# A decoder block on one core: fetching down rows block by block, four native score tiles, and row rings in two

## The chip, the cores and the metric

The kernel runs on one core of a Trainium2 chip. The metric is the time of one execution on the device in microseconds. Three runs of the kernel before took 2116.78, 2117.88 and 2124.81 us; the median is 2117.88.

## The reference

The layer has 256 tokens of 2048 features in fp32. An input projection feeds windowed attention and retention; gated, merged and projected, they are added to the residual `h`. What follows is the part that matters here, the retrieval of experts:

```
hn  = RMSNorm(h)
s   = (hn @ w_query) . sub_keys          # 8 heads, 2 halves, 128 keys each
top 16 of each half -> 256 sums -> best 16: 128 expert numbers ib and gates gb per token
u   = expert_down[ib]; act = gelu(hn . u)           # 16384 experts, rows of 2048
y   = sum over the 128 experts of gb * act * expert_up[ib]
out = RMSNorm(h + y)
```

## The kernel before, in words

Tokens lie on the partitions, in two blocks `b` of 128 (`NB`). Weights come in units of up to four 128 x 512 chunks through a ring of three `raw` tiles (queue of SyncE). For an fp32r product a unit is split: ScalarE casts it to `whi`, VectorE subtracts that into `wlo` (L107, L108), and TensorE multiplies three times per chunk and block (L138 to L140, L154 to L156). Each of these rings has three slots, so splits run at most three pairs of chunks ahead of TensorE.

After `w_out` come four query tiles (`w_q`), whose scores TensorE transposes and multiplies with the sub-keys (L498, L503). Then come 32 *score tiles* (`gemm1`, L463): each multiplies 512 expert rows with all tokens, over the first 11 of the 16 feature chunks only, 8 in fp32r and 3 in native fp32 from `raw` itself (L161, `htf` is the unsplit input). ScalarE scales the result into `a` (L467) and writes it to a score table in DRAM, `a_dram` (L468).

The last 5 chunks, 640 features, are not computed for all experts. When the experts of a token are known, GpSimd (POOL) fetches 640-feature pieces of their down rows with indirect DMAs, one row per token at a time (`fetch_u`, L605), and VectorE forms the dot product (`dot`, L613, `djunk`). There are 256 such steps, 128 per block. They need the routing of a block: `top16`, `candidates`, `cand_top`, `ranks` and `pick` on VectorE give the numbers `sel`, and `indices` (L586) turns them into row numbers `ix`. Before, `indices` runs once for both blocks. Each dot frees a slot of the ring of eight tiles `v` and issues the fetch eight further on; the last eight dots issue the first fetches of *up rows* (`fetch`, L583), which use the same ring.

What runs between the tiles is put on a list by `later` with a cost; `drain` takes entries off it when a unit of a product has been written, up to a budget for that unit (`BG_RATE`, `BG_NATIVE`). A scheduler then orders the instructions of each engine by a simulated timeline. On the chip each engine takes its list in that order.

In the last stage POOL gathers, per step, one score per token from `a_dram` (`score`, L640, `wsel`) and fetches an up row of 2048 features (L583); VectorE adds gate x gelu x row into `ys` (L689). Fourteen scores lead; the order of POOL's instructions is written out by `in_line`. `finish` normalises a block.

Of the kernel before, what the change touches and what calls it, by code (L numbers as in the profile page):

```python
# [26 lines left out]
NE = 16384  # L27
NT = NE // 512
BG_RATE = 2.8
BG_NATIVE = 4.9  # L30
CF = 8
CN = 3
CG = NC - CF - CN
GC = CG * P
G0 = D - GC
DOT = 0.85
VR = 8
GRP = 8
LEAD = 14

# [2 lines left out]
def hybrid_block(ctx, tc, x, x_t, anorm, fnorm, frow, w_in, w_ab, w_rb, w_out, w_q, skeys, down, down_n, down_g, up, sinks, fin,  # L43
# [24 lines left out]
        for j in range(4):  # L68
            units += [w[j, u] for u in range(4)]
    for t in range(NT):  # L70
        units += [down[t, u] for u in range(CF // 4)] + [down_n[t]]

    state = {"emitted": 0, "used": 0}
    bg = deque()
# [1 line left out]
    def later(cost, fn, *args):  # L76
        bg.append((cost, fn, args))
# [8 lines left out]
    ready = {}  # L86

    def emit_unit(u):
        if units[u].shape[1] == CN:
            nat = stream.tile([P, 4, 512], F32, name="raw", bufs=3)  # L90
            nc.sync.dma_start(nat[:, :CN], units[u])
            ready[u] = nat
            return
        raw = stream.tile([P, 4, 512], F32, name="raw", bufs=3)
        if u == 0:
            for i in range(4):
                nc.sync.dma_start(raw[:, i], units[u][:, i])
        else:
            nc.sync.dma_start(raw, units[u])
        hs = []  # L100
        for i in range(2):
            hi = stream.tile([P, 2, 512], F32R, name="whi", bufs=3)
            lo = stream.tile([P, 2, 512], F32R, name="wlo", bufs=3)
            step = 1 if u == 0 else 2
            for k in range(0, 2, step):
                src = raw[:, 2 * i + k:2 * i + k + step]
# [36 lines left out]

    def gemm_mixed(ops, xf):
        ps = [acc.tile([P, 512], F32, name="acc") for _ in range(NB)]
        for u in range(CF // 4):
            hs = next_unit()
            for k in range(4):
                hi, lo = hs[k // 2]
                wh, wl = hi[:, k % 2], lo[:, k % 2]  # L150
                c = u * 4 + k
                for b in range(NB):
                    xh, xl = ops(c, b)
                    nc.tensor.matmul(ps[b], lhsT=xh, rhs=wh, start=(c == 0), stop=False)  # L154
                    nc.tensor.matmul(ps[b], lhsT=xh, rhs=wl, start=False, stop=False)  # L155
                    nc.tensor.matmul(ps[b], lhsT=xl, rhs=wh, start=False, stop=False)  # L156
            drain(BG_RATE)
        nat = next_unit()
        for k in range(CN):
            for b in range(NB):  # L160
                nc.tensor.matmul(ps[b], lhsT=xf[:, k, b * P:(b + 1) * P], rhs=nat[:, k], start=False,  # L161
                                 stop=(k == CN - 1))
        drain(BG_NATIVE)
        return ps

    def pair_ops(hi, lo):
# [287 lines left out]

    peer = pool("peer")
    h_ops = pair_ops(hth, htl)
    htf = peer.tile([P, CN, T], F32, name="htf")
# [110 lines left out]
    for b in range(NB):  # L568
        later(2.0, candidates, b)
        for hd in range(8):  # L570
            later(1.0, cand_top, b, hd)
        later(2.0, ranks, b)
        later(4.6, pick, b, 0)
        later(4.6, pick, b, 1)
    ix = peer.tile([P, 2, NB, P], U32, name="ix")
    vtiles = {}
    vp = {}

    def fetch(n):
        v = vp["pool"].tile([P, D], F32, name="v", bufs=VR)  # L580
# [5 lines left out]
    def indices():  # L586
        rt.close()
        msk.close()
        tmp2 = pool("tmp2")
        ef = tmp2.tile([P, 2, NB, P], F32, name="ef")  # L590
        nc.vector.scalar_tensor_tensor(ef[:, 0], sel[:, 0], 128.0, sel[:, 1], op0=OP.mult, op1=OP.add)
        for b in range(NB):
            nc.vector.tensor_scalar_add(ef[:, 1, b], ef[:, 0, b], rows[:, b:b + 1])
        nc.vector.tensor_copy(ix, ef)
        vp["pool"] = pool("v")
        vp["ps"] = pool("ysum", space=PSUM)
        for n in range(VR):
            fetch_u(n)

    utiles = {}  # L600

    def fetch_u(n):
        u = vp["pool"].tile([P, D], F32, name="v", bufs=VR)
        b, k = divmod(n, P)
        nc.gpsimd.indirect_dma_start(u[:, :GC], None, down_g, IndirectOffsetOnAxis(ap=ix[:, 0, b, k:k + 1], axis=0),  # L605
                                     bounds_check=NE - 1)
        utiles[n] = u

    def dot(n):
        u = utiles.pop(n)  # L610
        b, k = divmod(n, P)
        junk = peer.tile([P, GC], BF16, name="djunk", bufs=2)
        nc.vector.scalar_tensor_tensor(junk, u[:, :GC], rstd2[:, b:b + 1], hg[:, b], op0=OP.mult, op1=OP.mult,  # L613
                                       accum_out=sdot[:, b, k:k + 1])
# [11 lines left out]
    fbc = peer.tile([P, D], F32, name="fbc")  # L626
    nc.scalar.dma_start(fbc, bass.AP(tensor=fin.tensor, offset=fin.offset, ap=[[0, P], [1, D]]))
# [67 lines left out]


# [62 lines left out]
```

## Time and profile before

| | us |
|---|---|
| median of three runs | 2117.88 |
| profiled execution | 2116.2 |
| its span, first to last instruction | 2114.4 |
| TensorE / VectorE / POOL busy | 1387.9 / 1556.2 / 918.4 |
| score tiles, first to last matmul | 873 to 1412 |
| down-row fetches, first to last issue | 963.2 to 1389.6 |
| last stage, first score issue to end | 1422 to 2114 |

Busy times are sums over the whole span. What an engine's time is worth differs from stage to stage, so the rows below are mostly of stretches. A busy TensorE is not TensorE at its peak: durations of matmuls overlap, and their pace is read from the distance of their starts.

### The profile page before, as it was taken

To read this page: it belongs to the slowest core of one execution; us is meant where nothing else is said; L and a number is where in the kernel's file an instruction comes from. 1 tells how busy PE (TensorE), PEld (TensorE's weight loads), DVE (VectorE), ACT (ScalarE), POOL (GpSimd) and SP (SyncE) were. 2 spreads that over 40 slices of the span, in tenths; PEclk is the share of its full clock that TensorE was granted. 3 is DMA by queue.
4 is the path that set the end of the run, shared out by engine and by line. 5 is a ranking of instruction groups with operands and counts; after the bars stand their busy time and mean duration, and the time that the engine had idled before them with its cause. 6 is when DMAs were issued, how large, how long until landed. Compare 5 with 4: busy or idle time off the path is not lost.

```text
span 2114.4 us, 18649 instructions
## 1 busy us (share of the span) xinstructions
PE 1387.9 (66%) x5864; PEld 1076.1 (51%) x5864; DVE 1556.2 (74%) x2037; ACT 614.7 (29%) x780; POOL 918.4 (43%) x802
## 2 busy tenths in 40 slices
PE   8999999999999999999999999960000000000000
PEld 6888888888888888866666676640000000000000
DVE  5676576544544567796777877748989899999998
ACT  6555444444444454433333333310000001000001
POOL 0101001000000000006888888857777777777773
PEclk9999999999999999999999999985555555555555
DMA  8545545655555564559999999987999999999997
GB/s 313 183 151 176 175 144 197 221 197 187 193 189 192 191 231 162 176 194 325 406 406 391 391 408 408 396 353 271 395 397 395 399 399 384 410 400 407 399 400 307
DMA packets 114516, 630.24 MB, mean 298 GB/s; under 512 B 21872, under 2 KB 22512, under 8 KB 54000
## 3 DMA queue, kind: packets, MB, share of 16 engines
q0 software_dynamic: 65536, 352.50, 42.3%
q1 hardware_dynamic: 38016, 253.77, 33.0%
q10 hardware_dynamic: 10864, 22.77, 2.8%
q8 instruction: 46, 0.75, 0.1%
q14 instruction: 54, 0.44, 0.1%
HBM read 610.10 MB, written 18.87 MB: 297 GB/s over the span
## 4 chain that ended last, share of the span: by engine, by line
PE 47%; DMA 20%; issue 17%; POOL 8%; DVE 8%; POOLq 0%; ACT 0%; ACTq 0%; DVEq 0%; SPq 0%
PE acc L139 13%; PE acc L138 13%; PE acc L140 13%; DMA v<-in_down_g_dram,ix 11%; DMA v<-in_up_dram,ix 6%; DVE ys L689 4%; POOL v L583 4%; POOL wsel L640 3%; PE acc L161 2%; DMA wsel<-a_dram,ix 2%; DVE wlo L108 1%; PE acc L155 1%; PE acc L156 1%; PE acc L154 1%; POOL v L605 1%
## 5 line engine op out<-in xcount | busy, mean ns | idle before, releaser
L108 DVE TENSOR_TENSOR wlo<-raw,whi 128x1024 fp32r<-128x1024 f32 (+1 forms) x426 | 526.1, 1236 | 332.9 <-ACT whi L107 332.5
L107 ACT CAST whi<-raw 128x1024 fp32r<-128x1024 f32 (+1 forms) x426 | 443.8, 1048 | 667.7 <-PE acc L140 367.5
L689 DVE SCALAR_TENSOR_TENSOR ys<-v,wsel,ys 128x2048 f32<-128x2048 f32 x254 | 598.3, 2355 | 30.8 <-DMA v<-in_up_dram,ix 23.3
L605 POOL DMA_INDIRECT v<-in_down_g_dram,ix x256 | 347.5, 1357 | 353.0 <-ACT whi L107 273.0
L640 POOL DMA_INDIRECT wsel<-a_dram,ix x256 | 259.1, 1012 | 96.4 <-issue 93.0
L583 POOL DMA_INDIRECT v<-in_up_dram,ix x256 | 260.9, 1019 | 80.7 <-issue 58.7
L613 DVE SCALAR_TENSOR_TENSOR djunk<-v,rs_r,hg 128x640 bf16<-128x640 f32 x256 | 219.2, 880 | 99.6 <-DMA v<-in_down_g_dram,ix 99.0
L139 PE MATMUL acc<-wlo,xth 128*128 128x512 f32 x736 | 291.9, 397 | 0.0
L140 PE MATMUL acc<-whi,xtl 128*128 128x512 f32 x736 | 288.2, 392 | 0.0
L138 PE MATMUL acc<-whi,xth 128*128 128x512 f32 x736 | 266.7, 394 | 9.1 <-ACT whi L107 9.1
L155 PE MATMUL acc<-wlo,hth 128*128 128x512 f32 x512 | 203.8, 398 | 13.1 <-DVE wlo L108 12.9
L156 PE MATMUL acc<-whi,htl 128*128 128x512 f32 x512 | 200.1, 391 | 0.0
L154 PE MATMUL acc<-whi,hth 128*128 128x512 f32 x512 | 191.4, 411 | 2.2 <-ACT whi L107 2.2
L681 ACT ACTIVATE wsel<-wsel 128x8 f32<-128x8 f32 x32 | 6.6, 208 | 595.9 <-DVE wsel L680 533.7
L161 PE MATMUL acc<-raw,htf 128*128 128x512 f32 x384 | 169.9, 592 | 0.0
L138 PEld LDWEIGHTS acc<-whi,xth 128*128 128x128 f32 x736 | 138.7, 189 | 38.3 <-ACT whi L107 9.5
L139 PEld LDWEIGHTS acc<-wlo,xth 128*128 128x128 f32 x736 | 138.8, 189 | 29.7 <-DVE wlo L108 1.0
L140 PEld LDWEIGHTS acc<-whi,xtl 128*128 128x128 f32 x736 | 138.8, 189 | 28.1 <-issue 0.2
L433 POOL TENSOR_TENSOR sg<-sg 128x512 f32<-128x512 f32 x8 | 14.1, 1790 | 291.8 <-DVE sg L432 291.8
L155 PEld LDWEIGHTS acc<-wlo,hth 128*128 128x128 f32 x512 | 96.1, 188 | 42.9 <-DVE wlo L108 22.2
L154 PEld LDWEIGHTS acc<-whi,hth 128*128 128x128 f32 x512 | 96.1, 188 | 33.5 <-issue 12.2
L161 PEld LDWEIGHTS acc<-raw,htf 128*128 128x128 f32 x384 | 72.7, 189 | 79.1 <-issue 76.6
(185 smaller groups left out, 1483.7 us busy)
## 6 DMA issues: line engine op xcount, KB each, us to landing
raw<-in_w_in_dram SPq DMA_DIRECT2D x91, 1024.0 KB, 4.8
raw<-in_down_dram SPq DMA_DIRECT2D x64, 1024.0 KB, 8.9
raw<-in_down_n_dram SPq DMA_DIRECT2D x32, 768.0 KB, 6.7
raw<-in_w_rb_dram SPq DMA_DIRECT2D x16, 1024.0 KB, 4.8
raw<-in_w_out_dram SPq DMA_DIRECT2D x16, 1024.0 KB, 4.8
raw<-in_w_q_dram SPq DMA_DIRECT2D x16, 1024.0 KB, 4.8
a_dram<-a ACTq DMA_DIRECT2D x32, 512.0 KB, 12.2
raw<-in_w_ab_dram SPq DMA_DIRECT2D x8, 1024.0 KB, 4.9
```

The lines of the kernel that those rows point to most:

```text
L107: nc.scalar.copy(hi[:, k:k + step], src)
L108: nc.vector.tensor_sub(lo[:, k:k + step], src, hi[:, k:k + step].bitcast(F32))
L138: nc.tensor.matmul(ps[b], lhsT=xh, rhs=wh, start=(c == 0), stop=False)
L139: nc.tensor.matmul(ps[b], lhsT=xh, rhs=wl, start=False, stop=False)
L140: nc.tensor.matmul(ps[b], lhsT=xl, rhs=wh, start=False, stop=(c == last))
L154: nc.tensor.matmul(ps[b], lhsT=xh, rhs=wh, start=(c == 0), stop=False)
L155: nc.tensor.matmul(ps[b], lhsT=xh, rhs=wl, start=False, stop=False)
L161: nc.tensor.matmul(ps[b], lhsT=xf[:, k, b * P:(b + 1) * P], rhs=nat[:, k], start=False, stop=(k == CN - 1))
L583: return nc.gpsimd.indirect_dma_start(v, None, up, IndirectOffsetOnAxis(ap=ix[:, 0, b, k:k + 1], axis=0), bounds_check=NE - 1)
L605: nc.gpsimd.indirect_dma_start(u[:, :GC], None, down_g, IndirectOffsetOnAxis(ap=ix[:, 0, b, k:k + 1], axis=0), bounds_check=NE - 1)
L640: return nc.gpsimd.indirect_dma_start(wsel[:, b, k:k + 1], None, a_flat, IndirectOffsetOnAxis(ap=ix[:, 1, b, k:k + 1], axis=0), bounds_che ...
L689: nc.vector.scalar_tensor_tensor(ys, v, w[:, kk:kk + 1], ys, op0=OP.mult, op1=OP.add)
```

## The change

Routing is finished block by block. `indices(b)` runs after each block's own picks; block 0's run starts the first fetches of down rows, and block 1's last score pieces (`held`) and routing steps are put behind it with a dot of block 0 after every second one. The row tiles are now two rings: `u`, nine slots of 640 features, and `v`, five slots of 2048, to which four more tiles (`more`, in the room of the split input) are added when the score tiles are done. The pool of `v` and the load of the final gain `fbc` are opened by `routed`, after block 1's routing.

All three units of the first four score tiles are native fp32. Of the other 28, a tile's third unit is native in 17 and split like the others in 11. For this `htf` has all 11 chunks and is summed on GpSimd. The costs and budgets on the list are set anew (`DOT`, 1.0 to 1.4 for the top-16 steps, 0.7 or 1.65 per chunk).

```diff
-BG_NATIVE = 4.9
-CF = 8
-CN = 3
+NATIVE_RATE = 1.65
+CD = 11
+ALL_NATIVE = 4
-DOT = 0.85
-VR = 8
+DOT = 0.95
+UR = 9
+VR = 5
...
+    native = set()
+    base = len(units) - 3 * NT
+    for t in range(NT):
+        kinds = range(3) if t < ALL_NATIVE else (2,) if (t - ALL_NATIVE) % 5 in (0, 2, 4) else ()
+        native.update(base + 3 * t + k for k in kinds)
...
+                    if u in native:
+                        nc.tensor.matmul(ps[b], lhsT=xf[:, c, b * P:(b + 1) * P], rhs=w[:, k], start=first, stop=last)
+                        continue
...
+            drain(n * (NATIVE_RATE if u in native else BG_RATE / 4))
...
-    nc.vector.tensor_add(htf, hth[:, CF:CF + CN].bitcast(F32), htl[:, CF:CF + CN].bitcast(F32))
+    for c in range(0, CD, 4):
+        e = min(c + 4, CD)
+        nc.gpsimd.tensor_add(htf[:, c:e], hth[:, c:e].bitcast(F32), htl[:, c:e].bitcast(F32))
...
-            later(1.0, top16, top[:, b, 4 * j + i], topi[:, b, 4 * j + i], sc[:, i])
+            item = (1.4, top16, top[:, b, 4 * j + i], topi[:, b, 4 * j + i], sc[:, i])
+            if b and j == 3:
+                held.append(item)
+            else:
+                later(*item)
...
-        u = vp["pool"].tile([P, D], F32, name="v", bufs=VR)
+        u = peer.tile([P, GC], F32, name="u", bufs=UR)
...
-        if n + VR < NB * P:
-            fetch_u(n + VR)
-        else:
-            fetch(n + VR - NB * P)
-
-    later(4.0, indices)
-    for n in range(NB * P):
+        if n + UR < NB * P:
+            fetch_u(n + UR)
+        elif 0 <= n + UR - NB * P < VR:
+            fetch(n + UR - NB * P)
+
+    def indices(b):
...
+        nc.vector.tensor_copy(ix[:, :, b], ef)
+        if b == 0:
+            for n in range(UR):
+                fetch_u(n)
...
+    done = 0
+    for b in range(NB):
+        steps = held if b else []
+        steps.append((2.0, candidates, b))
+        steps += [(1.4, cand_top, b, hd) for hd in range(8)]
+        steps += [(2.0, ranks, b), (4.6, pick, b, 0), (4.6, pick, b, 1), (1.0, indices, b)]
+        for i, st in enumerate(steps):
+            later(*st)
+            if b and i % 2:
+                later(DOT, dot, done)
+                done += 1
+    later(0.0, routed)
+    for n in range(done, NB * P):
         later(DOT, dot, n)
...
+    more = [keep.tile([P, 2, D], F32, name=f"more_{t}", tag=t) for t in ("xh", "xl")]
+    vp["more"] = [m[:, i] for m in more for i in range(2)]
...
+    for n in range(VR, VR + 4):
+        in_line(fetch, n)
...
-                if n + VR < total:
-                    in_line(fetch, n + VR)
+                if n + VR + 4 < total:
+                    in_line(fetch, n + VR + 4)
```

The scheduler's order shows three places. On POOL, from the last sums of the mixers to the start of the last stage, before:

```order
L433 TENSOR_TENSOR sg<-sg 128x512 x8
L605 DMA v<-in_down_g_dram,ix 128x640 x256
L583 DMA v<-in_up_dram,ix 128x2048 x8
L640 DMA wsel<-a_dram,ix 128x1 x15
L583 DMA v<-in_up_dram,ix 128x2048
```

and after:

```order
L440 TENSOR_TENSOR sg<-sg 128x512 x8
L467 TENSOR_TENSOR htf<-hth,htl 128x1024 x2
L467 TENSOR_TENSOR htf<-hth,htl 128x768
L602 DMA u<-in_down_g_dram,ix 128x640 x19
L594 DMA v<-in_up_dram,ix 128x2048 x5
L602 DMA u<-in_down_g_dram,ix 128x640 x237
L666 DMA wsel<-a_dram,ix 128x1 x14
L594 DMA more_xh<-in_up_dram,ix 128x2048 x2
L594 DMA more_xl<-in_up_dram,ix 128x2048 x2
L666 DMA wsel<-a_dram,ix 128x1
```

The sums for `htf` are new, five up rows have moved from behind the down rows to the 20th place, and four stand behind the leading scores.

On VectorE, the last dots (`djunk`) among the splits of weights (`wlo`), up to the first sum of the last stage, before:

```order
L613 SCALAR_TENSOR_TENSOR djunk,sdot<-v,rs_r,hg 128x640 x4
L108 TENSOR_TENSOR wlo<-raw,whi 128x1024
L613 SCALAR_TENSOR_TENSOR djunk,sdot<-v,rs_r,hg 128x640
L108 TENSOR_TENSOR wlo<-raw,whi 128x1024
L613 SCALAR_TENSOR_TENSOR djunk,sdot<-v,rs_r,hg 128x640 x3
L108 TENSOR_TENSOR wlo<-raw,whi 128x1024 x2
L680 TENSOR_TENSOR wsel<-wsel,sdot 128x8
L682 TENSOR_TENSOR wsel<-wsel,sel 128x8
L687 TENSOR_SCALAR ys<-v,wsel 128x2048
```

and after:

```order
L610 SCALAR_TENSOR_TENSOR djunk,sdot<-u,rs_r,hg 128x640 x6
L115 TENSOR_TENSOR wlo<-raw,whi 128x1024
L610 SCALAR_TENSOR_TENSOR djunk,sdot<-u,rs_r,hg 128x640
L115 TENSOR_TENSOR wlo<-raw,whi 128x1024
L610 SCALAR_TENSOR_TENSOR djunk,sdot<-u,rs_r,hg 128x640 x3
L115 TENSOR_TENSOR wlo<-raw,whi 128x1024 x3
L115 TENSOR_TENSOR wlo<-raw,whi 128x512
L115 TENSOR_TENSOR wlo<-raw,whi 128x1024 x13
L115 TENSOR_TENSOR wlo<-raw,whi 128x512
L115 TENSOR_TENSOR wlo<-raw,whi 128x1024 x4
L708 TENSOR_TENSOR wsel<-wsel,sdot 128x8
```

The last dot has moved from in front of the last two splits to in front of the last 22; counted from the end, these are the splits of tiles 28 to 31 (18) and four of the six of tile 27.

On TensorE, in the first score tile, the last query scores (`qs`, `sk`) among its products, before (the end of the piece):

```order
L155 MATMUL acc<-wlo,hth 128x512
L156 MATMUL acc<-whi,htl 128x512
L154 MATMUL acc<-whi,hth 128x512
L155 MATMUL acc<-wlo,hth 128x512
L156 MATMUL acc<-whi,htl 128x512
L154 MATMUL acc<-whi,hth 128x512
L155 MATMUL acc<-wlo,hth 128x512
L156 MATMUL acc<-whi,htl 128x512
L161 MATMUL acc<-raw,htf 128x512 x6
L503 MATMUL ms<-sk,qt 128x128 x4
L154 MATMUL acc<-whi,hth 128x512
L155 MATMUL acc<-wlo,hth 128x512
```

and after (the whole piece):

```order
L162 MATMUL acc<-raw,htf 128x512 x10
L507 MATMUL ms<-ident,qs 128x128 x4
L162 MATMUL acc<-raw,htf 128x512 x10
L512 MATMUL ms<-sk,qt 128x128 x4
L507 MATMUL ms<-ident,qs 128x128 x4
L162 MATMUL acc<-raw,htf 128x512 x10
L512 MATMUL ms<-sk,qt 128x128 x4
L162 MATMUL acc<-raw,htf 128x512 x54
L166 MATMUL acc<-whi,hth 128x512 x2
```

The transposes and key products of the query scores have moved in between native matmuls.

## Rows read from the trace of the kernel before

**Rows 1.** Busy time by stage (us, counts), the columns in the first row.

```profile
core 0: us, PE busy (x) PEld busy (x) DVE busy (x) ACT busy (x) POOL busy (x), PEclk, DMA share, GB/s
873.00:963.00 90.00, 87.78 (x344) 62.21 (x343) 81.17 (x268) 34.35 (x41) 0.00 (x0) 1.00 0.58 190
963.00:1398.00 435.00, 421.94 (x1553) 289.99 (x1552) 331.62 (x615) 141.06 (x156) 353.33 (x261) 1.00 1.01 397
1413.00:1442.00 29.00, 0.00 (x0) 0.00 (x0) 6.66 (x5) 1.52 (x3) 15.21 (x16) 0.54 0.24 92
1442.00:2088.00 646.00, 0.00 (x0) 0.00 (x0) 598.54 (x328) 13.04 (x44) 494.32 (x489) 0.50 1.01 397
```

**Rows 2.** Chain that ended last, share of the span by line.

```profile
PE acc L139 13%; PE acc L138 13%; PE acc L140 13%; DMA v<-in_down_g_dram,ix 11%; DMA v<-in_up_dram,ix 6%; DVE ys L689 4%; POOL v L583 4%; POOL wsel L640 3%; PE acc L161 2%; DMA wsel<-a_dram,ix 2%; DVE wlo L108 1%; PE acc L155 1%; PE acc L156 1%; PE acc L154 1%; POOL v L605 1%
```

**Rows 3.** ScalarE's timeline (start us, us, operation): results of tiles 6 and 31.

```profile
993.94 0.69 ACT L467 ACTIVATE a<-acc,rs_r 128x512 f32<-128x512 f32 x1 [6.78 <-PE acc L161]
...
1411.48 0.69 ACT L467 ACTIVATE a<-acc,rs_r 128x512 f32<-128x512 f32 x1 [11.40 <-PE acc L161]
1412.34 0.69 ACT L467 ACTIVATE a<-acc,rs_r 128x512 f32<-128x512 f32 x1 [0.17 <-PE acc L161]
```

**Rows 4.** TensorE's timeline in tile 0, fp32r and native.

```profile
880.62 0.39 PE L155 MATMUL acc<-wlo,hth 128*128 128x512 f32 x1
...
881.75 0.39 PE L154 MATMUL acc<-whi,hth 128*128 128x512 f32 x1
...
885.85 5.31 PE L161 MATMUL acc<-raw,htf 128*128 128x512 f32 x12
891.00 1.05 PE L503 MATMUL ms<-sk,qt 128*128 128x128 f32 x8
```

**Rows 5.** Tile v: ns min/median/max, first and last start us.

```profile
L605 POOL DMA_INDIRECT v<-in_down_g_dram,ix x256: 1007/1307/2168, 963.2 to 1389.6; - x128
L613 DVE SCALAR_TENSOR_TENSOR djunk<-v,rs_r,hg x256: 869/880/908, 971.5 to 1397.0; 128x640 bf16<-128x640 f32 x128
L583 POOL DMA_INDIRECT v<-in_up_dram,ix x256: 1000/1010/1641, 1391.0 to 2086.7; - x128
```

**Rows 6.** POOL's timeline: first fetch, one beside splits, first score, last stage.

```profile
963.22 2.17 POOL L605 DMA_INDIRECT v<-in_down_g_dram,ix  x1 [273.05 <-ACT whi L107]
...
1311.58 1.84 POOL L605 DMA_INDIRECT v<-in_down_g_dram,ix  x1 [0.30 <-DVE djunk L613]
...
1422.22 1.02 POOL L640 DMA_INDIRECT wsel<-a_dram,ix  x1 [18.69 <-issue]
...
1606.68 1.01 POOL L640 DMA_INDIRECT wsel<-a_dram,ix  x1 [0.30 <-issue]
```

**Rows 7.** Line 154, first and last start.

```profile
L154 PE MATMUL acc<-whi,hth x512: 387/389/793, 873.1 to 1406.3; 128*128 128x512 f32 x171
```

**Rows 8.** Groups of the page: a sum on POOL.

```profile
L433 POOL TENSOR_TENSOR sg<-sg 128x512 f32<-128x512 f32 x8 | 14.1, 1790 | 291.8 <-DVE sg L432 291.8
```

**Rows 9.** ScalarE's timeline: block 0's last query scores.

```profile
883.07 0.59 ACT L505 COPY sc<-ms 128x512 f32<-128x512 f32 x1
```

**Rows 10.** Busy time of all engines while VectorE routes.

```profile
884.00:962.20 78.20, 75.98 (x283) 52.26 (x282) 75.82 (x264) 27.04 (x33) 0.00 (x0) 1.00 0.58 188
```

**Rows 11.** Busy time of VectorE's splits (L108) in that stretch.

```profile
884.00:962.20 78.20, 20.81 (x18) 1.00 0.58 188
```

**Rows 12.** Busy time in ten microseconds, the fastest among the dots.

```profile
1200.00:1210.00 10.00, 9.44 (x38) 6.82 (x37) 9.22 (x19) 2.28 (x3) 8.17 (x7) 1.00 1.02 418
```

**Rows 13.** Groups of the page: splits on VectorE.

```profile
L108 DVE TENSOR_TENSOR wlo<-raw,whi 128x1024 fp32r<-128x1024 f32 (+1 forms) x426 | 526.1, 1236 | 332.9 <-ACT whi L107 332.5
```

**Rows 14.** VectorE's timeline beside that fetch.

```profile
1311.31 1.22 DVE L108 TENSOR_TENSOR wlo<-raw,whi 128x1024 fp32r<-128x1024 f32 x1
```

**Rows 15.** Result writes, from issue to landing.

```profile
DMA to landing us min/median/max: 6.4/12.2/14.6
```

**Rows 16.** Busy time of POOL's down-row fetches (L605) among the dots.

```profile
963.00:1398.00 435.00, 347.51 (x256) 1.00 1.01 397
```

More of the change, by code (lines that the diff above doesn't have):

```diff
@@ L70, in hybrid_block @@
     for t in range(NT):
-        units += [down[t, u] for u in range(CF // 4)] + [down_n[t]]
+        units += [down[t, 0], down[t, 1], down_n[t]]
+    native = set()
[3 more added lines that the diff above has]
+        native.update(base + 3 * t + k for k in kinds)
     state = {"emitted": 0, "used": 0}
@@ L88, in emit_unit @@
     def emit_unit(u):
[L89 to L93, printed above, removed]
         raw = stream.tile([P, 4, 512], F32, name="raw", bufs=3)
+        n = units[u].shape[1]
         if u == 0:
@@ L98, in emit_unit @@
         else:
-            nc.sync.dma_start(raw, units[u])
+            nc.sync.dma_start(raw[:, :n], units[u])
+        if u in native:
+            ready[u] = raw
+            return
         hs = []
-        for i in range(2):
+        for i in range(0, n, 2):
             hi = stream.tile([P, 2, 512], F32R, name="whi", bufs=3)
             lo = stream.tile([P, 2, 512], F32R, name="wlo", bufs=3)
-            step = 1 if u == 0 else 2
-            for k in range(0, 2, step):
-                src = raw[:, 2 * i + k:2 * i + k + step]
+            m = min(2, n - i)
+            step = 1 if u == 0 else m
+            for k in range(0, m, step):
+                src = raw[:, i + k:i + k + step]
                 nc.scalar.copy(hi[:, k:k + step], src)
@@ L145, in gemm_mixed @@
         ps = [acc.tile([P, 512], F32, name="acc") for _ in range(NB)]
[L146 to L151, printed above, removed]
+        c = 0
+        for _ in range(3):
+            u = state["used"]
+            n = units[u].shape[1]
+            w = next_unit()
+            for k in range(n):
+                first, last = c == 0, c == CD - 1
                 for b in range(NB):
+                    if u in native:
+                        nc.tensor.matmul(ps[b], lhsT=xf[:, c, b * P:(b + 1) * P], rhs=w[:, k], start=first, stop=last)
+                        continue
+                    wh, wl = (v[:, k % 2] for v in w[k // 2])
                     xh, xl = ops(c, b)
-                    nc.tensor.matmul(ps[b], lhsT=xh, rhs=wh, start=(c == 0), stop=False)
+                    nc.tensor.matmul(ps[b], lhsT=xh, rhs=wh, start=first, stop=False)
                     nc.tensor.matmul(ps[b], lhsT=xh, rhs=wl, start=False, stop=False)
[L156 to L163, printed above, removed]
+                    nc.tensor.matmul(ps[b], lhsT=xl, rhs=wh, start=False, stop=last)
+                c += 1
+            drain(n * (NATIVE_RATE if u in native else BG_RATE / 4))
         return ps
@@ L456, in hybrid_block @@
     h_ops = pair_ops(hth, htl)
-    htf = peer.tile([P, CN, T], F32, name="htf")
-    nc.vector.tensor_add(htf, hth[:, CF:CF + CN].bitcast(F32), htl[:, CF:CF + CN].bitcast(F32))
+    htf = peer.tile([P, CD, T], F32, name="htf")
+    for c in range(0, CD, 4):
+        e = min(c + 4, CD)
+        nc.gpsimd.tensor_add(htf[:, c:e], hth[:, c:e].bitcast(F32), htl[:, c:e].bitcast(F32))
     a_dram = dram.tile([T, NE], F32, name="a_dram")
@@ L566, in pick @@
         nc.vector.tensor_add(sel[:, s, b].rearrange("p (h k) -> p h k", h=8), oh[:, :, 0], oh[:, :, 1])
[L568 to L574, printed above, removed]
     ix = peer.tile([P, 2, NB, P], U32, name="ix")
@@ L579, in fetch @@
     def fetch(n):
-        v = vp["pool"].tile([P, D], F32, name="v", bufs=VR)
+        r = n % (VR + 4)
+        if r < VR:
+            v = vp["pool"].tile([P, D], F32, name="v", bufs=VR)
+        else:
+            v = vp["more"][r - VR]
         b, k = divmod(n, P)
@@ L584, in fetch @@
                                             bounds_check=NE - 1)
[L586 to L598, printed above, removed]
     utiles = {}
     def fetch_u(n):
-        u = vp["pool"].tile([P, D], F32, name="v", bufs=VR)
+        u = peer.tile([P, GC], F32, name="u", bufs=UR)
         b, k = divmod(n, P)
-        nc.gpsimd.indirect_dma_start(u[:, :GC], None, down_g, IndirectOffsetOnAxis(ap=ix[:, 0, b, k:k + 1], axis=0),
+        nc.gpsimd.indirect_dma_start(u, None, down_g, IndirectOffsetOnAxis(ap=ix[:, 0, b, k:k + 1], axis=0),
                                      bounds_check=NE - 1)
@@ L612, in dot, with routed @@
         junk = peer.tile([P, GC], BF16, name="djunk", bufs=2)
-        nc.vector.scalar_tensor_tensor(junk, u[:, :GC], rstd2[:, b:b + 1], hg[:, b], op0=OP.mult, op1=OP.mult,
+        nc.vector.scalar_tensor_tensor(junk, u, rstd2[:, b:b + 1], hg[:, b], op0=OP.mult, op1=OP.mult,
                                        accum_out=sdot[:, b, k:k + 1])
-        if n + VR < NB * P:
-            fetch_u(n + VR)
-        else:
-            fetch(n + VR - NB * P)
-    later(4.0, indices)
-    for n in range(NB * P):
+        if n + UR < NB * P:
[3 more added lines that the diff above has]
+    def indices(b):
+        ef = rp.tile([P, 2, P], F32, name="ef")
+        nc.vector.scalar_tensor_tensor(ef[:, 0], sel[:, 0, b], 128.0, sel[:, 1, b], op0=OP.mult, op1=OP.add)
+        nc.vector.tensor_scalar_add(ef[:, 1], ef[:, 0], rows[:, b:b + 1])
+        nc.vector.tensor_copy(ix[:, :, b], ef)
+        if b == 0:
+            for n in range(UR):
+                fetch_u(n)
+    def routed():
+        rt.close()
+        msk.close()
+        vp["pool"] = pool("v")
+        vp["ps"] = pool("ysum", space=PSUM)
+        fbc = vp["pool"].tile([P, D], F32, name="fbc")
+        nc.scalar.dma_start(fbc, bass.AP(tensor=fin.tensor, offset=fin.offset, ap=[[0, P], [1, D]]))
+        vp["fbc"] = fbc
+    done = 0
[11 more added lines that the diff above has]
+    for n in range(done, NB * P):
         later(DOT, dot, n)
```

11 lines of the change are left out of this document (5 added, 6 removed).

## Prediction

> **What bounds the kernel now.** I read four views in turn: busy time by stage, the chain of waits, the timelines of the engines that meet in the score stage, and the groups by line. The windows [rows 1] split the end of the kernel. From 873 to 963 us (score tiles, routing on VectorE) the DMA engines are 58% busy at 190 GB/s. From 963 to 1398 us, while the dots run, they are at 1.01 and 397 GB/s. From 1413 to 1442 us they are nearly idle, and from 1442 to 2088 us again at 1.01. In the chain [rows 2], fetches of down rows hold 11% of the span and native matmuls 2%: in the score stage the arrival of rows ends last.
>
> Two paces confirm it. Between the results of tiles 6 and 31, at 993.94 and 1411.48 us [rows 3], a tile takes 417.5 / 25 = 16.70 us. TensorE alone needs less: six fp32r matmuls start between 880.62 and 881.75 us, 0.226 us apart; twelve native pieces, six matmuls, take 891.00 - 885.85 = 5.15 us, 0.858 us each [rows 4]. A tile of 8 fp32r chunks and 3 native ones (3 products x 2 blocks, or 1 x 2) needs 48 x 0.226 + 5.15 = 16.0 us. With 10 dots a tile, a tile moves 2.88 MB of weights, 0.52 MB of results and 10 x 0.328 MB of rows: 6.69 MB, at 16.70 us 400 GB/s, the DMA engines' pace. POOL is as full: 256 issues start between 963.2 and 1389.6 us [rows 5], 1.67 us each, with only 0.3 us between two. In the last stage POOL paces too: a score and an up row at 1.01 us each plus two 0.3 us gaps are 2.62 us a row [rows 6].
>
> **The change: native tiles.** They cost TensorE nothing in sum: a native tile takes 22 x 0.858 = 18.9 us, an all-fp32r one 66 x 0.226 = 14.9. Of the others 17 stay mixed and 11 become all-fp32r: 4 x 18.9 + 17 x 16.0 + 11 x 14.9 = 511.5 us, against 32 x 16.0 = 512. VectorE's splits only move: none for the first four tiles, 134 instead of 128 later (11 of them half size). Tile 0 starts at 873.1 us [rows 7]; with 2 us of query transposes, tile 4 starts at 950.7. The sums for TensorE's input on POOL: two of 1024 columns and one of 768 at 1.79 us per 512 [rows 8] are 9.8 us, in the 70 us of query projection in which POOL idles; uncovered, at most 9.8 us.
>
> **Earlier fetches.** Routing waits for the last query scores, and on TensorE their transposes and products now stand behind ten native matmuls each: 8.6 us twice instead of the mixture now, so the copy at 883.07 us [rows 9] comes at about 892. From 884 to 962.2 us VectorE is busy for 75.8 us [rows 10], of them 20.8 in 18 splits [rows 11]; 55 are routing. The splits go, and about 7 us of block 1's last picks come after block 0's indices, so these exist at 892 + 48 = 940 us and the first fetch starts at about 941.5, instead of 963.2 [rows 6]: 22 us earlier. I add nothing for ScalarE, where the load of the final gain now waits behind six casts for the end of routing; it may cost 0 to 5 us.
>
> **What the order makes of them.** VectorE takes its list in order, and a tile's splits stand behind the dots written before them. Before: 10 dots to a tile, through tile 31. After: about 11 to a tile from tile 4 on, the last one between the second and third split of tile 27, with 22 splits and no dot behind it. So TensorE can't pass tile 27 until all 256 rows have come. On POOL the first 5 up rows stand after 19 fetches and must land meanwhile too. Bytes from 941.5 us (tile 3.5) to that dot: rows 83.9 MB, up rows 5.2, 23.7 tiles x 3.41 = 80.8: 169.9 MB. The prices:
> - DMA at the stage's pace of 400 GB/s: 425 us, to 1366.
> - DMA at the best ten microseconds among the dots, 418 GB/s [rows 12]: 406 us, to 1348.
> - POOL at its present 1.67 us: 261 issues are 435 us, to 1376, and 8 us to land and be used (as from 1389.6 to 1397.0 [rows 5]): 1384.
>
> I take the first, since its row covers the whole stage and before's pace agrees with it: last dot at 1367 us. VectorE needs 256 x 0.88 us for dots [rows 5] and about 112 x 1.24 for splits [rows 13], 364 of the 416 us to there, so it does not set the end but has little slack. Behind the last dot TensorE has 13.4 us of tile 27 and tiles 28 to 31, 16.0 + 16.0 + 14.9 + 16.0: 76.3 us, to 1443.5, against 1412.3 [rows 3]: +31 us. The gain at the front (22 us of fetching) is spent by tile 27, and in the last five tiles DMA, with nothing but weights to carry, runs at some 220 GB/s: the idle stretch has moved from the front to the back and grown.
>
> A rule is to be weighed here. Beside a split at 1311.31 us [rows 14] the POOL issue of 1311.58 took 1.84 us; in the last stage one takes 1.01 [rows 6]. The Trainium skill (SBUF — State Buffer, "SBUF: two separate sides") says that VectorE and GpSimd share an SBUF port pair that one instruction holds as a whole, VectorE also when it has two inputs in SBUF, and the other waits. Splits and dots both have two, and by that rule 11 dots and 4.8 splits a tile lengthen issues further: the last dot would come at POOL's 1384 or later, 17 us behind mine.
>
> **The last stage.** The final result's DMA now shares the engines with no up rows (8 before, 5 early now). Results land after 6.4 us at best [rows 15]; before, POOL resumed at 1422.22 us [rows 6], 9.2 after the issue: -2.8 us. Then 256 scores and 251 up rows instead of 248: 3 x 1.31 = +3.9. Four of them go out before the first sum, but POOL's list, not the ring, sets the pace. If DMA paced the stage, three rows would cost 3 x 2.62 = 7.9. Both are at their limit there, so I take the middle of -2.8 + 3.9 = 1.1 and -2.8 + 7.9 = 5.1: +3.
>
> **Sum.** 31 + 3 = +34 us on the 2116.2 us of the profiled execution (its span of 2114.4 and 1.8 around it), 2150; the median of the runs lies 1.7 above that execution, so 2152.
>
> **Rivals.**
> - *TensorE paces it.* If rows always came in time, the score stage would end at 873.1 + 2 + 511.5 = 1386.6, 25.7 us earlier; with +3 the median is 2095, faster. For it: before 963 us the DMA engines leave 90 x (1 - 190 / 400) = 47 us unused, nine slots instead of eight. Against: from tile 4 to 27, 251 dots and 23 tiles in 23 x 15.6 us are 160.6 MB in 359 us, 447 GB/s, and no ten microseconds among the dots reach over 418. It decides from a feed of some 445 GB/s, or if fetching starts 50 us earlier.
> - *DMA gives more than now,* at 418 GB/s: 19 us less, 2133; what lies between this and the first rival belongs here. For it: deeper rings, better filled. The Trainium skill (DMA: Bandwidth & Descriptors, "Measured") gives 425 GB/s for 16 MB; by that my sum would lose an estimated 25 us. No row here holds that for long.
> - *POOL paces the dots:* at its present pace the last dot is at 1384, 17 us later: 2169. If what lengthens an issue (347.5 / 256 = 1.36 us against 1.01 [rows 16]) grows with VectorE's busy share, from 331.6 / 435 = 76% [rows 1] to 364 / 416 = 88%, each takes 0.06 us more, 15 us in all: 2184.
> - *The fetches don't start earlier,* because VectorE mixes both blocks' routing: 22 us more, 2174.
>
> **Chances.** Forecast (DMA pace, 2134 to 2168) 0.58; POOL or late fetches, 2168 to 2184, 0.14; more bandwidth, 2108 to 2134, 0.16; TensorE paces, about 2095, 0.12. A measurement can tell 0.5%, 10.6 us: faster is below 2107, slower above 2128.5. Faster 0.12; same, most of the bandwidth case, 0.13; slower 0.75. The range leaves out the TensorE case and the far ends: 2112 to 2182.
>
> **What would show it.** Right: first fetch near 941 us; DMA at 1.0 from there to about 1367; tiles 4 to 27 some 17.5 to 18 us apart; no dot in tiles 28 to 31, these 15 to 16 us apart at about 220 GB/s; TensorE's end near 1443; the last stage as long as before. Wrong: tiles 4 to 27 at 15 to 16 us, which would be the first rival, or dots that end later than 1385, which would be the third.

## The result, and the profile after

The changed kernel takes 2177.1 us (four runs, 2173.77 to 2180.23) where the kernel before takes 2117.3 on the same chip: a ratio of 1.0277, 95% interval 1.0246 to 1.0308, some 60 us slower. The forecast was 2152, 35 us slower. The measured time lies inside the range given (2112 to 2182), near its upper end, and outside the 2134 to 2168 that the forecast's own term was given: in the band for "POOL or late fetches", which had a chance of 0.14.

The windows by stage are read first, as [rows 1] were, now cut at the first fetch, the last dot and TensorE's end:

```profile
core 0: us, PE busy (x) PEld busy (x) DVE busy (x) ACT busy (x) POOL busy (x), PEclk, DMA share, GB/s
873.00:947.00 74.00, 74.00 (x199) 35.50 (x198) 49.41 (x241) 9.32 (x16) 0.00 (x0) 1.00 0.46 160
947.00:1397.00 450.00, 390.83 (x1469) 277.36 (x1468) 344.16 (x638) 143.32 (x162) 350.78 (x261) 0.96 0.99 381
1397.00:1472.00 75.00, 74.39 (x296) 55.11 (x294) 26.26 (x24) 26.39 (x31) 0.00 (x0) 1.00 0.53 181
1472.00:2120.00 648.00, 0.00 (x0) 0.00 (x0) 581.10 (x317) 14.34 (x45) 491.75 (x488) 0.50 0.98 387
```

The new row is the third. For 75 us behind the last dot TensorE works without a pause, POOL issues nothing, and the DMA engines are half empty. In the second row it is the other way round: the transfers are full and TensorE, busy for 97% of the time among the dots before [rows 1], is busy for 87%. Work that ran side by side stands one after the other.

Tile u's groups (instruction: ns min/median/max, first and last start) answer to [rows 5]:

```profile
L602 POOL DMA_INDIRECT u<-in_down_g_dram,ix x256: 1007/1307/2022, 947.6 to 1388.4; - x128
L610 DVE SCALAR_TENSOR_TENSOR djunk<-u,rs_r,hg x256: 866/880/948, 952.5 to 1396.8; 128x640 bf16<-128x640 f32 x128
```

The fetches begin 15.6 us earlier, and the last dot starts at 1396.8 us, where it started before (1397.0). ScalarE's timeline of results of tiles 4, 26 and 31, counted from 0 as in [rows 3]:

```profile
978.17 0.69 ACT L476 ACTIVATE a<-acc,rs_r 128x512 f32<-128x512 f32 x1 [6.83 <-PE acc L162]
...
1390.45 0.69 ACT L476 ACTIVATE a<-acc,rs_r 128x512 f32<-128x512 f32 x1 [12.28 <-PE acc L162]
...
1470.57 0.69 ACT L476 ACTIVATE a<-acc,rs_r 128x512 f32<-128x512 f32 x1 [11.40 <-PE acc L162]
1471.42 0.69 ACT L476 ACTIVATE a<-acc,rs_r 128x512 f32<-128x512 f32 x1 [0.17 <-PE acc L162]
```

The last result comes at 1471.4, 59.1 us after that of before, and from there to the end of the span it is 704.8 us against 702.1: 59.1 + 2.7 = 61.8, the whole difference of the two spans (2176.2 - 2114.4). So the loss lies in the score stage (873 us to TensorE's end).

One hole is in it as well. POOL's timeline where the first five up rows (line 594) stand between down rows:

```profile
980.64 1.31 POOL L594 DMA_INDIRECT v<-in_up_dram,ix  x1 [0.30 <-issue]
...
986.18 1.69 POOL L594 DMA_INDIRECT v<-in_up_dram,ix  x1 [0.30 <-issue]
988.17 1.90 POOL L602 DMA_INDIRECT u<-in_down_g_dram,ix  x1 [0.30 <-DVE djunk L610]
...
998.83 1.01 POOL L602 DMA_INDIRECT u<-in_down_g_dram,ix  x1 [3.96 <-DMA v<-in_up_dram,ix]
```

VectorE's timeline, the dot that waits for the row fetched at 988.17; and all engines while it waits:

```profile
1009.56 0.88 DVE L610 SCALAR_TENSOR_TENSOR djunk<-u,rs_r,hg 128x640 bf16<-128x640 f32 x1 [17.05 <-DMA u<-in_down_g_dram,ix]
```

```profile
1000.00:1010.00 10.00, 0.00 (x0) 0.00 (x0) 0.44 (x1) 0.73 (x1) 2.61 (x3) 0.50 1.02 416
```

The row lands 21 us after its issue. The transfers are full (416 GB/s), but of bytes that nobody needs yet; the splits written behind that dot wait with it, TensorE stands still, and its granted clock falls to 0.50, the lower of its two levels. So the result of tile 6 comes 34.0 us behind that of tile 5:

```profile
996.03 1.27 ACT L476 ACTIVATE a<-acc,rs_r 128x512 f32<-128x512 f32 x2 [5.73 <-PE acc L168]
...
1030.00 0.69 ACT L476 ACTIVATE a<-acc,rs_r 128x512 f32<-128x512 f32 x1 [5.96 <-PE acc L162]
```

### The profile page after: what moved, and what is told of

Its sections match the earlier page's. It is cut to its first block, busy times and chain, and to the rows that moved or that the text cites. A ratio compares the mean times of both kernels' runs of the same rounds, so it can differ in the third digit from the quotient of the medians.

```text
span 2176.2 us, 18678 instructions
## 1 busy us (share of the span) xinstructions
PE 1402.9 (64%) x5866; PEld 1081.3 (50%) x5866; DVE 1562.7 (72%) x2044; ACT 613.2 (28%) x786; POOL 921.0 (42%) x805
## 4 chain that ended last, share of the span: by engine, by line
PE 33%; issue 26%; DMA 22%; DVE 12%; POOL 6%; ACT 0%; POOLq 0%; SPq 0%; ACTq 0%; DVEq 0%
DMA u<-in_down_g_dram,ix 12%; PE acc L146 10%; PE acc L147 10%; PE acc L145 10%; DVE ys L717 9%; DMA wsel<-a_dram,ix 6%; DMA v<-in_up_dram,ix 2%; POOL wsel L666 2%; POOL u L602 2%; POOL v L594 1%; DVE djunk L610 1%; DMA more_xl<-in_up_dram,ix 1%; DVE wlo L115 1%; DMA more_xh<-in_up_dram,ix 1%; POOL more_xl L594 1%
## 5 line engine op out<-in xcount | busy, mean ns | idle before, releaser
L602 POOL DMA_INDIRECT u<-in_down_g_dram,ix x256 | 344.8, 1347 | 250.2 <-DVE ix L621 160.9
L717 DVE SCALAR_TENSOR_TENSOR ys<-v,wsel,ys 128x2048 f32<-128x2048 f32 x142 | 334.5, 2356 | 5.0
L610 DVE SCALAR_TENSOR_TENSOR djunk<-u,rs_r,hg 128x640 bf16<-128x640 f32 x256 | 219.2, 881 | 89.9 <-DMA u<-in_down_g_dram,ix 89.6
L166 PE MATMUL acc<-whi,hth 128*128 128x512 f32 x514 | 186.8, 404 | 10.1 <-ACT whi L114 10.1
L594 POOL DMA_INDIRECT v<-in_up_dram,ix x144 | 145.5, 1011 | 45.3 <-issue 33.5
L717 DVE SCALAR_TENSOR_TENSOR ys<-more_xl,wsel,ys 128x2048 f32<-128x2048 f32 x56 | 131.9, 2356 | 2.0
L717 DVE SCALAR_TENSOR_TENSOR ys<-more_xh,wsel,ys 128x2048 f32<-128x2048 f32 x56 | 131.9, 2356 | 1.9
```

Of the source, the lines that this page charges most:

```text
L602: nc.gpsimd.indirect_dma_start(u, None, down_g, IndirectOffsetOnAxis(ap=ix[:, 0, b, k:k + 1], axis=0), bounds_check=NE - 1)
L610: nc.vector.scalar_tensor_tensor(junk, u, rstd2[:, b:b + 1], hg[:, b], op0=OP.mult, op1=OP.mult, accum_out=sdot[:, b, k:k + 1])
```

## The experiments

All twelve are compared with the kernel before as it ran beside them on the same chip, since its time differs from one set of runs to the next: it took 2153.7 us beside e1 to e4, 2156.9 beside e5 to e8, 2117.7 beside e9 to e12. What differs is the last stage (see the end of this text); the last score result of the changed kernel comes at 1471.4 us in its first trace and at 1474.8 in e5, so times inside the score stage are quoted from all sets, with such a difference in mind. Theories: Q, the order of dots on VectorE (11 a tile, ending at tile 27) exposes the tail; D, transfers set the rows' pace; P, POOL's issues do; N, the new shares of native and fp32r pieces slow the tiles.

**e1: the five up rows behind the last down row.**

```
         elif 0 <= n + UR - NB * P < VR:
-            fetch(n + UR - NB * P)
+            with tc.issue_after(vp["last_u"].ins):
+                fetch(n + UR - NB * P)
```

> The five early up-row fetches are queued behind the last down-row fetch; nothing else is changed. Theory Q (the up rows stand in POOL's queue in front of the next down row, which lands 21 us after its issue instead of 8, and everything behind the dot stands still): the 32 us between the results of tiles 5 and 6 shrink to about 17, the last dot comes some 15 us earlier than 1396.8 us, the time is 2160 to 2165 us. Rival (only their five issues cost, at POOL's pace of 1.66 us each): 8 us less, 2169. Rival (something else holds tile 6): no change, 2177.

Ratio 1.0200 (1.0183 to 1.0217), against 1.0262 (1.0236 to 1.0288) for the changed kernel in e5: some 13 us back. The hole is gone (tile 6 follows tile 5 after 15.8 us, in the changed kernel 34.0), and the last dot starts at 1380.1:

```profile
L602 POOL DMA_INDIRECT u<-in_down_g_dram,ix x256: 1011/1304/2067, 945.4 to 1370.2; - x128
L610 DVE SCALAR_TENSOR_TENSOR djunk<-u,rs_r,hg x256: 865/882/949, 950.3 to 1380.1; 128x640 bf16<-128x640 f32 x128
```

The rows keep their pace, (1370.2 - 945.4) / 255 = 1.67 us, and from the last dot to the last result (1462.8) there are 83 us of bare weights. That is what the first theory expected. So the up rows are some fifth of the loss, not its core.

**e2: as e1, and each dot kept behind the newest split,** so that the dots reach tile 31 (a dot's cost on the list, `DOT`, is 1.03).

```
+        with tc.issue_after(state["split"].ins):
             nc.vector.scalar_tensor_tensor(junk, u, rstd2[:, b:b + 1], hg[:, b], ...
```

> As e1, and every dot is queued behind the newest split written before it, with 1.03 instead of 0.95 as its cost on the list, so that the dots lie at 7 to 11 a tile up to tile 31 instead of 11 a tile up to tile 27. Theory (11 rows a tile are more than the feed gives, and behind the last dot TensorE works alone on four tiles while DMA idles): at 9.2 rows a tile and 1.66 us a row a tile needs 15.3 us, TensorE's own pace; no dead tail; the score stage ends near 1400 us instead of 1472 and the time is 2100 to 2115 us. Rival (the density of the dots doesn't matter, TensorE's end follows the start of the fetches and the native tiles): about e1's time, 2160 or more.

1.0150 (1.0133 to 1.0167). The tail is gone, 10 us from the last dot to the last result, but the tiles take 17.0 us and tiles 4 and 5 25 each, and the last result comes at 1442.9. Far above what was expected: with the tail away, something else holds the tiles.

**e3: as e2 in dense order, every row at half its bytes,** 320 features read twice by the dot, so that the other 320 are left out (`DOT` is 0.86).

```
-        u = peer.tile([P, GC], F32, name="u", bufs=UR)
+        u = peer.tile([P, GC // 2], F32, name="u", bufs=UR)
```

> As e1, but each fetch brings 320 of the 640 features (the dot reads these twice; the second half of the features is left out), with 256 fetches and dots as before, ordered at about 11 a tile up to tile 27. Theory D (DMA bandwidth paces the fetches): 42 MB less, fetches come every 1.42 us or less, TensorE paces the tiles at 15.6 us, the last dot comes before 1330 us, the time is 2090 to 2105 us. Theory P (POOL's issuing paces them, whatever their size): still 1.6 to 1.7 us a fetch, last dot at 1370 to 1385 us, 2145 to 2165 us.

1.0188 (1.0171 to 1.0205). POOL in 300 us among the dots (busy time, count, clock, DMA share, GB/s):

```profile
core 0: us, POOL busy (x), PEclk, DMA share, GB/s
1030.00:1330.00 300.00, 244.83 (x182) 0.98 0.85 290
```

The transfers have room (0.85), and a row still takes 300 / 182 = 1.65 us: 244.83 / 182 = 1.345 for the issue and the 0.3 us gap. The last dot starts at 1372.9. Both are as P expected; D alone is out.

**e4: in the kernel before, the dots' operand hg copied to PSUM.**

```
-        ... rstd2[:, b:b + 1], hg[:, b], op0=OP.mult, ...
+        ... rstd2[:, b:b + 1], vp["hg"][:, b * GC:(b + 1) * GC], op0=OP.mult, ...
```

> The kernel before, with the dots' second input (hg) copied to PSUM, so that a dot has one input in SBUF. Theory L (a POOL issue waits while VectorE runs an operation with two inputs in SBUF): the mean issue falls from 1.36 us to 1.15 or less, a row then comes every 1.60 us, which is TensorE's pace at ten dots a tile, the score stage ends 10 to 18 us earlier: 2100 to 2107 us. Rival (issues are lengthened by something else, or DMA paces the fetches): issues of 1.3 to 1.4 us or no gain in time, 2113 to 2121 us.

0.9991 (0.9980 to 1.0003): no difference. Tile v's group, beside the 1307 ns of [rows 5]:

```profile
L608 POOL DMA_INDIRECT v<-in_down_g_dram,ix x256: 1009/1015/2140, 963.9 to 1381.9; - x128
```

The median issue loses 0.29 us when the dot has one SBUF operand. By the port rule weighed in the prediction (the Trainium skill, SBUF — State Buffer, "SBUF: two separate sides") it should, and the trace agrees. The rows come 1.64 us apart instead of 1.67, the tiles take 16.4 us instead of 16.70, and the last result comes at 1405.9, 6.4 us ahead of that in the trace of before, which is of another set; the times show no gain clear of noise. At 10 rows a tile the transfers are full (1.02, 406 GB/s between 1030 and 1330) and TensorE is busy for 99%; that these two hold the tiles now is argued from these numbers, not tried.

**e5: the changed kernel itself,** as a yardstick for the next three.

> The changed kernel itself, as a yardstick beside the three others on the same chip. Theory Q (the dots written 11 to a tile and ending at tile 27 leave four tiles of bare weights behind the last row, while the rows keep coming at 1.66 us each) and theory N (the new shares of native and fp32r pieces are what slows the tiles) both expect the ratio already seen, 1.025 to 1.031, with the last dot some 75 us ahead of TensorE's end.

1.0262 (1.0236 to 1.0288), last dot at 1400.2, last result at 1474.8.

**e6: the old shares of arithmetic in every tile.**

```
-        kinds = range(3) if t < ALL_NATIVE else (2,) if (t - ALL_NATIVE) % 5 in (0, 2, 4) else ()
+        kinds = (2,)
```

> The changed kernel with the old shares of arithmetic: the third unit of every tile native, the other two fp32r. Dots still 10 to 11 a tile, the last one in tile 28; the five up rows still stand early on POOL. Theory Q: rows at 1.66 us each as in the changed kernel, last dot at about 1395 us, behind it 3.5 tiles of 16 us, TensorE's end near 1452 and 20 us off the changed kernel: ratio 1.018 to 1.022. Theory N: tiles back at 16.5 us from end to end, TensorE's end near 1415, ratio 1.000 to 1.005.

1.0214 (1.0193 to 1.0236), a ratio as Q expected, though the last dot (1404.1) and the last result (1463.0) come some 10 us later than written. N as the main cause is out. Against e5 the old shares give 12 us at the last result and some 10 in the time, where the intervals touch.

**e7: old shares, late up rows, 9 to 11 dots a tile to tile 31.** e1's, e2's and e6's edits, DOT = 1.12, and

```
-            if b and i % 2:
-                later(DOT, dot, done)
+            for _ in range(2 if b else 0):
+                later(0.5, dot, done)
```

> The changed kernel with all three suspects out: old shares of arithmetic in every tile, the five up rows behind the last down row, and each dot kept behind the newest split, 9 to 11 a tile from tile 5 to tile 31; the early routing, the rings and the rest of the change stay. If theory N holds (two thirds of what the even order with the new shares still lost is the shares), the tiles take 16.2 us, TensorE ends at 942 + 28 x 16.2 = 1396, 16 us before the kernel before: ratio 0.990 to 0.997. If the shares cost nothing, it repeats the ratio of the even order with the new shares, 1.013 to 1.017.

1.0049 (1.0032 to 1.0066), between the two expectations. With every suspect out the kernel is nearly back, though its fetches start 11 us before those of [rows 6]: most of its tiles from the 13th on take 16.4 or 17.7 us. Against e2 it is 22 us faster, and 19 of them are there by the result of tile 5 (982.3, in e2 1001.0), so the four native tiles cost more here than in e6; but two dots instead of one behind every routing step changed as well, and no run parts the two.

**e8: the kernel before, with nothing but the order of dots and splits fixed** at 11 to 12 dots a tile, three in tile 28, none behind (`DOT` is 0.92).

```
+                with tc.issue_after(state["dot"]) if "dot" in state else nullcontext():
+                    state["split"] = nc.vector.tensor_sub(lo[:, k:k + step], src, ...
...
+        with tc.issue_after(state["split"].ins):
+            state["dot"] = nc.vector.scalar_tensor_tensor(junk, u[:, :GC], ...
```

> The kernel before with one thing altered: the order of dots and splits on VectorE is fixed at 11 to 12 dots a tile, from tile 6 to tile 27 and three in tile 28, instead of 10 a tile to tile 31. Theory Q: the rows come no faster (1.66 us each), so the last dot stays at 1395 to 1400, and 3.8 tiles of 16 us stand behind it: TensorE's end at 1458, 46 us late, ratio 1.020 to 1.024. Theory N, for which the order is harmless and the shares are the cause: ratio 0.998 to 1.005. Theory D (the rows would come faster if the dots asked for them, up to the transfers' pace): last dot at 1350 to 1360, TensorE's end at 1412 to 1420, ratio 1.000 to 1.004.

1.0180 (1.0158 to 1.0202), 39 us slower. Tile v's groups, and the stretches before and behind the last dot:

```profile
L607 POOL DMA_INDIRECT v<-in_down_g_dram,ix x256: 1006/1300/2038, 966.4 to 1383.6; - x128
L616 DVE SCALAR_TENSOR_TENSOR djunk<-v,rs_r,hg x256: 871/884/947, 971.2 to 1392.4; 128x640 bf16<-128x640 f32 x128
```

```profile
1230.00:1330.00 100.00, 92.81 (x337) 63.92 (x336) 75.16 (x146) 29.01 (x32) 81.00 (x62) 0.98 1.00 386
1330.00:1400.00 70.00, 63.90 (x230) 44.95 (x230) 51.80 (x96) 19.66 (x22) 54.10 (x42) 0.95 1.00 387
1400.00:1450.00 50.00, 47.14 (x168) 32.24 (x167) 14.35 (x12) 16.10 (x18) 0.00 (x0) 0.97 0.79 308
```

This is the plainest result. Asked for 11.4 rows a tile in place of 10, the rows come hardly faster (1.636 us apart, before 1.672), so the last dot moves by 5 us only, and the weights of the last four tiles stand bare behind it: last result at 1458.9. (The 308 GB/s in the last stretch are these weights and the first eight up rows, issued from 1385.5 on.) ScalarE's list, which matters in e12 below, is not the cause here: ScalarE waits in front of its result copies for 29 us between 1030 and 1330, before for 37. The order alone makes two thirds of the loss. Singly measured, the order (39 us), the up rows (13) and the shares (10) add up to 62, near the 60 of the whole change; that they add in this way is not shown, for taken out of the changed kernel the dense order gives back only 11 us (e1 to e2), other waits coming in its place.

**e9, e10, e11: what sets the 1.64 us.** e8 with hg in PSUM (e4's edit), with half rows (e3's, which leave out features), and with both.

> The kernel before with the dense order of dots (11 to 12 a tile to tile 27, as in the run before), and the gain-times-state operand of the dots copied to PSUM, so that a dot reads one operand from SBUF and lengthens no issue on POOL. In the dense order the rows came 1.636 us apart. Theory P (POOL's issues, 1.36 + 0.3 us beside dots with two SBUF operands, set it): mean issue falls to 1.2 as in the even order, rows 1.50 to 1.57 us apart (then TensorE's 16.0 / 11.4 = 1.40 and the transfers' 7.15 MB / 11.4 at 400 GB/s = 1.57 are next), last dot at 1355 to 1375, TensorE's end 17 to 35 us ahead of the dense order without it. Theory D (transfers): 1.63 to 1.65 as there, last dot at 1390. Theory V (VectorE's list with its waits): 1.63 too.

> The dense order again, every down row cut to half its bytes (320 of the 640 features; the dot reads them twice, so the second half of these features is left out); the operand stays in SBUF. A tile moves 5.28 MB instead of 7.15. Theory P: rows still 1.62 to 1.66 us apart, last dot at 1385 to 1395, DMA busy 0.85. Theory D: the transfers are out of the way, rows at TensorE's 1.40 to 1.45 us, last dot at 1335.

> Both at once: dense order, half rows (second half of the features left out), operand in PSUM. Theory P: rows 1.40 to 1.50 us apart, last dot at 1330 to 1355. If P and D bind in turn (whichever is relieved alone leaves the other), the two single runs stay above 1.57 and only this one comes to 1.40 to 1.45. Theory V: 1.63 in all three.

Ratios 1.0104 (1.0085 to 1.0122), 1.0109 (1.0087 to 1.0130) and 0.9954 (0.9939 to 0.9969). POOL among the dots, one fence for each, in this order:

```profile
1030.00:1330.00 300.00, 216.24 (x191) 0.98 1.01 398
```

```profile
1030.00:1330.00 300.00, 243.28 (x187) 0.97 0.82 294
```

```profile
1030.00:1330.00 300.00, 234.40 (x206) 0.99 0.88 319
```

Read each as 300 / count against busy / count + 0.3. With half rows (second): 1.604 and 1.601, POOL never rests. With the operand in PSUM (first): 1.571 and 1.432, POOL has 0.14 us to spare, and the transfers are full at 398 GB/s. With both (third): 1.456 and 1.438, POOL again, at its shorter issue. The last dots start at 1377.1, 1373.8 and 1346.0 in e10, e9 and e11. e9 and e11 are close to what P expected, e10 a little quicker (1.62 to 1.66 was written); V, for which nothing changes, is out. Two limits lie within 0.1 us of each other; taking one away leaves the other, and only both together quicken the rows much, which is the second alternative written down for e11, but for the 1.456 (1.40 to 1.45 was written).

e11 also tells what the stage could give. Rows of half the bytes and short issues keep TensorE 98% busy from 970 to 1400 us, yet its last result is at 1410.9, where the kernel before has 1412.3; the earliest of all runs is that of e4, 1405.9. So none of these edits takes more than some 6 us off the score stage of before. Whether another order could is open: where TensorE never waits, tiles take 16.1 us (e12 below), before 16.70.

**e12: as e7, but each dot kept behind the split before the newest,** so that dots may stand between a unit's two splits.

```
-        with tc.issue_after(state["split"].ins):
+        with tc.issue_after(state["prev"].ins):
```

> The changed kernel with the old shares, the up rows late and 9 to 11 dots a tile as in the run that measured 1.0049, but each dot kept behind the split before the newest only, so that dots may stand between the two splits of a unit instead of both splits standing side by side with seven dots behind them. If that clumping is what made its tiles 17.0 us where the kernel before takes 16.7, they take 16.3 to 16.6, TensorE ends 12 to 20 us earlier and the ratio is 0.995 to 0.999. If not (rows and weights come no faster with this ring), it repeats 1.003 to 1.007.

1.0154 (1.0140 to 1.0168): neither, and slower than e7. Its trace shows why, in two stretches of one run. First all engines, then ScalarE in each:

```profile
1030.00:1130.00 100.00, 100.00 (x369) 69.24 (x368) 75.10 (x140) 32.85 (x36) 76.64 (x59) 1.00 1.02 405
1180.00:1380.00 200.00, 185.52 (x659) 125.46 (x658) 132.97 (x248) 58.52 (x66) 135.06 (x104) 0.97 0.97 354
```

```profile
1079.01 1.99 ACT L114 CAST whi<-raw 128x1024 fp32r<-128x1024 f32 x2 [8.38 <-DMA raw<-in_down_dram]
1082.03 0.69 ACT L477 ACTIVATE a<-acc,rs_r 128x512 f32<-128x512 f32 x1 [1.03 <-PE acc L163]
...
1280.31 0.69 ACT L477 ACTIVATE a<-acc,rs_r 128x512 f32<-128x512 f32 x1 [11.82 <-PE acc L163]
1280.89 1.98 ACT L114 CAST whi<-raw 128x1024 fp32r<-128x1024 f32 x2
```

In the first stretch the casts for the next tile stand ahead of the copy of this tile's result, TensorE never waits, and tiles take 16.1 us. In the second the copy stands first; ScalarE takes its list in order, waits 11.8 us for the tile's last matmul, and the casts come behind it, so TensorE waits at each such tile: 18 to 20.5 us. One such wait, on TensorE:

```profile
1262.39 0.73 PE L167 MATMUL acc<-whi,hth 128*128 128x512 f32 x2 [1.71 <-ACT whi L114]
```

Behind it the granted clock is lower for some us (0.91 in the mean from 1262 to 1282), which adds to the tile. The new edges on VectorE had moved ScalarE's list too. ScalarE waits in front of that copy for 121 us between 1030 and 1330 in e12, 82 in e7, 76 in e2, 155 in e6, 37 in the kernel before. That this is what e2 and e7 still lost is read from the traces; no run of its own tried it. In the changed kernel itself it is 91 us and in e1 22, at one pace of the rows, so there it decided nothing. e1's edit, too, moved more than its five fetches.

No version that does the whole work beat the kernel before: e4 equals it, and e11 leaves work out.

## Why the prediction was right in sign and short in size

- **The tail: right.** 76.3 us forecast from the last dot to TensorE's end, 1471.4 - 1396.8 = 74.6 measured, the last tiles 15 to 16 us apart at 181 GB/s (some 220 forecast; nothing waits for it). e8 makes such a tail by the order alone.
- **Last dot at 1367: the step that failed, by 30 us.** "I take the first", it said, the transfers at 400 GB/s. Rows came 1.65 us apart at 386 GB/s (300 / 182 between 1030 and 1330), POOL's issue (1.336) and gap; e9 to e11 show both limits within 0.1 us. So it was the third rival that came, POOL's pace, priced at 2169 to 2184. That the time fell between these two is in part luck: the rival's last dot, 1384, was passed by 13 us through the late start and the up rows, and the longer issues that make its 2184 did not come. The row for it, 1.67 us in [rows 5], stood in the sum's own list, as did its warning that VectorE's denser work would lengthen issues. The issues did not lengthen: mean 344.8 / 256 = 1.35 us against 1.36 [rows 16]; there was simply no room to shorten a row's time.
- **The five up rows: mis-sized.** Counted as 5.2 MB, 13 us of transfers. They hold the queue: the next row lands 21 us after its issue, and the last dot moves by 1396.8 - 1380.1 = 16.7 us (e1, in another set of runs). The dots wait, then the splits behind them.
- **First fetch: 947.6, not 941.5.** The gain is 15.6 us of the 22 forecast. Block 0's last score copy came at 897.8 (892 forecast); the routing behind it, to the row numbers at 947.0, took 49 us (48 forecast). So the 6 us lie ahead of the routing, where query products and native matmuls alternate on TensorE.
- **Native tiles cost TensorE nothing in sum: about right.** Tile 4's first split product starts at 953.5 (950.7 forecast). But the sum leaves out what stands behind them: tile 4's splits stand behind dots that wait for the first rows (TensorE waits 5.0 us for one up to 965.61), so tile 4's first result comes at 978.3 in e5 and at 960.2 in e6. Of these 18 us 12 are left at the last result; e2 and e7 differ by 20 there. So what was put at nothing cost some 10 us by e6, whose interval touches that of e5.
- **Last stage +3: right,** 2.7 measured.
- **More bandwidth: did not come.** The Trainium skill (DMA: Bandwidth & Descriptors, "Measured") gives 425 GB/s for 16 MB; the most that 100 us of any run here show is 410 (e12, 980 to 1080 us), and the changed kernel has 386 at a share of 1.00.
- **What the prediction left out:** ScalarE's list. Apart from the load of the final gain (0 to 5 us) the prediction followed VectorE, POOL and TensorE, and the order of casts and copies on ScalarE changed as well. It cost the changed kernel nothing that shows, being behind POOL's pace, and it cost the variants that took that pace away.

Sum: the forecast's 2150 for the profiled execution, 30 for the last dot (6 for the late start, 4 for what the hole took beyond its bytes, and as the remainder 20 for POOL's pace, the 8 us from the last issue to the last dot, and whatever the native tiles cost), 2 less for the tail: 2178, which is what that execution took (2178.0).

## What to carry to other kernels

Where an engine takes its list in order, a stream of small operations should be spread over the whole of the work that it runs beside: asking for more of them per tile brings them no sooner when their feed is at its limit, and whatever is left without them at the end runs alone. Before trusting one pace, compare all that come within a few per cent; here POOL's issue, the transfers and TensorE did, and removing one showed the next. And after any edit of order read the lists of all engines, since a copy that slips ahead of two casts cost 2 to 4 us a tile here.

## What the runs showed of the hardware that was not expected

- Halving a row's bytes took the DMA share from 1.00 at 386 GB/s (changed kernel) to 0.85 at 290 (e3): the rate fell by 25%, the share by 15%. Here short rows occupy the engines for longer than in proportion to their bytes.
- Fetches issued behind five up rows of 1 MB each did not pass them: 21 us to land instead of some 8, and the issues themselves wait for those rows (3.96 us at 998.83).
- One program differs by 1.7 to 1.9% between sets of runs (2117 us beside the first result and e9 to e12, 2154 to 2157 beside e1 to e8), more than half of the effect studied here. The difference lies in the last stage: from the last score result to the end the changed kernel takes 704.8 us in its first trace and 739.1 in e5, with the transfers at 401 and 380 GB/s from 1500 to 2060. First its first trace, then e5:

```profile
1500.00:2060.00 560.00, 0.00 (x0) 0.00 (x0) 514.93 (x284) 12.32 (x40) 427.05 (x424) 0.50 1.01 401
```

```profile
1500.00:2060.00 560.00, 0.00 (x0) 0.00 (x0) 491.24 (x270) 11.91 (x38) 405.23 (x401) 0.50 0.98 380
```

e4 and e8 have 375 and 376 GB/s there, e9 and e12 401. Why is open; e1 to e4 and e9 to e12 carry the same chip number, so the number alone does not tell.
